# Three groups of products and the residual stream with tokens on partitions instead of features

## The chip, the core and the metric

One core of a Trainium2 chip runs the whole program; the other cores are idle. The metric is the device time of one execution in microseconds (us). The engines have short names: PE is TensorE's matrix products, PEld its loads of standing tiles, DVE is VectorE, ACT is ScalarE, POOL is GpSimd, SP is the queue that issues the weight loads.

## What is computed

Two layers of an encoder over 256 tokens of 2048 features, all float32. Each layer reads the residual stream x twice and adds to it twice:

```python
for l in range(DEPTH):                       # DEPTH = 2
    u = rmsnorm(x, norm_mix[l])
    proj = u @ w_in[l]
    c_q, c_kv, k_pe, q_na, k_na, v_na, gate_a, gate_b = jnp.split(proj, IN_SPLITS, axis=-1)
    ...                                      # latent attention and neighbourhood attention
    y_a = mla_attention(...) @ w_o_mla[l]    # 1024 -> 2048
    y_b = neighbourhood_attention(...) @ w_o_na[l]
    merged = jax.nn.sigmoid(gate_a) * y_a + jax.nn.sigmoid(gate_b) * y_b
    x = x + merged @ w_out[l]                # 2048 -> 2048
    h = rmsnorm(x, norm_mlp[l]) @ w_ff1[l]   # 2048 -> 8192
    x = x + jnp.square(jax.nn.relu(h)) @ w_ff2[l]   # 8192 -> 2048
return rmsnorm(x, norm_final)
```

## The kernel before

An activation is held with features on partitions: 128 features by 256 tokens, split exactly into a float32r part hi and the rest lo, side by side in one tile of 512 columns (`pair`, L76; `split`, L140). A weight is loaded in strips of two times 128 rows by 512 columns (`weights`, L149): one load of 1 MB on SP's queue for two strips, then ACT makes the hi part of a strip (L164) and DVE the lo part (L165). There are three buffers for loads and four for split strips. Every product is the sum of hi times hi, hi times lo and lo times hi.

`gemm_b` (L210) makes 512 output features from all rows of a weight. The weight's 128 by 128 tile stands in the array and the activation streams past it: one instruction with the weight's hi and 512 columns (hi and lo of the 256 tokens, L186) and one with the weight's lo and 256 columns (L187). I call these two **a pair**; a strip is eight pairs, in four blocks m of 128 output features. The two halves of the result are added by ACT and DVE (`whole`, L203), and `evac` uses the sum. Banks of PSUM: five for products, three (`abank`) for attention, transposes and norms.

`mm_a` (L192) is the other way round, used before only for the values v: a 128 by 128 tile of the activation (hi or lo, one block t of 128 tokens) stands and 512 columns of the weight stream past it, in three instructions (L194 to L196), **a triple**. The result has tokens on partitions and nothing is left to add.

x is kept as 16 tiles `xT` of features by tokens. Its first transposes are those of the input (`enter`, L393), its last those of the output (`turned`, L572). RMSNorm's scale of a token is applied to a product's result as a row `mix.row` or `mlp.row` along the free axis, which `Norm.scales` (L241) makes with small products (L245, L259).

The order on each engine is set by a scheduler that simulates the program while it is built; the program hands it work in the order in which it is written. Steps of attention heads and norms are generators: `tick()` (L111), called after each block of a product, advances one of them when its lag has passed, and `drain()` runs all that is left. Engines work in order, so what stands at the head of an engine's row holds up what is behind it.

Of the kernel before, what the change touches and what calls it, by code (L numbers as in the profile page):

```python
# [44 lines left out]
# columns of w_in  # L45
# [3 lines left out]
# columns of the gains' tile  # L49
G_MIX, G_MLP, G_FIN, G_QA, G_KVA, G_ALL = 0, 2 * NC, 4 * NC, 5 * NC, 5 * NC + 8, 5 * NC + 16  # L50

# buffers: operands of 2 KiB a partition, PSUM banks for attention, small temporaries, loaded
# strips of weights, split ones
NSLOT, ABANKS, SMALL, RBUFS, HBUFS = 47, 3, 8, 3, 4
# steps of a large product: between an attention head's start and the next one's, after its
# scores, after its transposes
# [4 lines left out]
def trunk(ctx: ExitStack, tc: tile.TileContext, x, w_in, w_uq, w_ukv, rpb, w_o_mla, w_o_na,  # L61
          w_out, w_ff1, w_ff2, gains, cos, sin, turns, halves, mask, out):
# [42 lines left out]
    xT = [const.tile([P, S], F32, name=f"xT{c}") for c in range(NC)]  # L105
# [34 lines left out]
    def split(dst, src, scale=1.0):  # L140
        """dst[:, :256] = float32r(src * scale), dst[:, 256:] = src * scale - that."""
# [26 lines left out]
    def weights_twice(w, nk, c0, n):  # L168
        """All rows of columns c0.. of w, each column twice over, eight times 128 rows a strip."""
# [19 lines left out]
    def mm_d(ps, wh, wl, a, first, last):  # L189
        mm_3(ps[:, :S], wh, wl, a[:, :S], a[:, S:], first, last)  # L190

    def mm_a(ps, a, t, wh, wl, first, last):  # L192
        """ps = a(token block t).T @ weights."""
# [16 lines left out]
    def gemm_b(w, c0, acts, evac, before=None, ahead=None, direct=False):  # L210
# [15 lines left out]
    class Norm:  # L226
# [14 lines left out]
        def scales(self, rows=True):  # L241
# [9 lines left out]
            if not rows:  # L251
                return
# [442 lines left out]
```

## Time and profile before

| | us |
|---|---|
| time, median of 3 runs | 2723.74 (2723.41 to 2723.89) |
| span of the profiled execution, first to last instruction | 2721.4 |
| PE busy in it | 2700.0 |
| PEld busy | 2363.2 |
| DVE busy | 1741.9 |
| ACT busy | 1408.5 |

The page gives no time of its own for the profiled execution, only its span; the runs' median lies 2.3 us above that. PE's busy time is made of instructions that overlap, so how long one takes is read from the distance between starts, and not from its own length.

### The profile page before, as it was taken

How to read it: one execution, taken by the hardware profiler on the slowest of the kernel's cores; microseconds unless marked ns; L12 is line 12 of the kernel's file. 1: busy time of each engine (PE TensorE's matmuls, PEld its weight loads, DVE VectorE, ACT ScalarE, POOL GpSimd, SP SyncE). 2: the span in 40 equal slices, each digit the busy share in tenths (PEclk: the TensorE clock that was granted, in tenths of full speed). 3: DMA queues.
4: the chain of work that ended last, by engine and by line, in shares of the span. 5: the costliest groups of instructions: out<-in, count | busy, mean ns of one | idle time of the engine just before them, and what ended most of it. 6: DMA issues, size and time to landing. Idle time of an engine off the chain costs nothing.

```text
span 2721.4 us, 39453 instructions
## 1 busy us (share of the span) xinstructions
PE 2700.0 (99%) x15608; PEld 2363.2 (87%) x15608; DVE 1741.9 (64%) x2649; ACT 1408.5 (52%) x2279; POOL 125.0 (5%) x153
## 2 busy tenths in 40 slices
PE   8999999999999999999999999999999999999998
PEld 7888898888888888888888888988888888888887
DVE  6676587666656556556667765876666556565564
ACT  5555465555544445445555554655555454454554
POOL 3110000001000000000101100000100000000001
PEclk9999999999999999999999999999999999999999
DMA  7555544555555555555555555455555555556553
GB/s 228 182 172 185 185 159 155 186 171 187 187 200 179 199 190 179 194 184 187 187 186 182 168 181 183 132 186 186 186 186 186 189 183 195 177 186 201 174 198 124
DMA packets 253545, 495.78 MB, mean 182 GB/s; under 512 B 12625, under 2 KB 16721, under 8 KB 253361
## 3 DMA queue, kind: packets, MB, share of 16 engines
q1 hardware_dynamic: 250624, 488.14, 54.8%
q0 software_dynamic: 1728, 3.51, 0.5%
q8 instruction: 122, 2.00, 0.3%
q10 hardware_dynamic: 1008, 1.62, 0.2%
q14 instruction: 63, 0.51, 0.1%
HBM read 491.14 MB, written 2.10 MB: 181 GB/s over the span
## 4 chain that ended last, share of the span: by engine, by line
PE 97%; issue 1%; DVE 1%; DMA 0%; ACT 0%; POOL 0%; POOLq 0%; ACTq 0%; DVEq 0%
PE bank L186 60%; PE bank L187 30%; PE bank L194 1%; PE bank L195 1%; PE bank L196 1%; PE abank L200 1%; PE abank L199 1%; PE abank L201 1%; PE abank L303 1%; DVE lo L165 0%; DMA raw<-in_w_in 0%; PE abank L273 0%; DMA wide<-in_x 0%; PE abank L401 0%; PE abank L259 0%
## 5 line engine op out<-in xcount | busy, mean ns | idle before, releaser
L186 PE MATMUL bank<-pair,hi 128*128 128x512 f32 x7040 | 2443.3, 397 | 4.2 <-DVE pair L146 3.9
L187 PE MATMUL bank<-pair,lo 128*128 128x256 f32 x7040 | 1893.0, 281 | 0.0
L165 DVE TENSOR_TENSOR lo<-raw,hi 128x1024 fp32r<-128x1024 f32 (+1 forms) x928 | 1122.3, 1222 | 804.0 <-ACT hi L164 801.6
L186 PEld LDWEIGHTS bank<-pair,hi 128*128 128x128 f32 x7040 | 1306.3, 188 | 282.6 <-DVE pair L146 4.2
L164 ACT CAST hi<-raw 128x1024 fp32r<-128x1024 f32 (+1 forms) x928 | 956.6, 1047 | 956.0 <-PE bank L186 888.1
L187 PEld LDWEIGHTS bank<-pair,lo 128*128 128x128 f32 x7040 | 1330.9, 189 | 35.1 <-DVE lo L165 0.2
L207 DVE TENSOR_TENSOR small<-bank,small 128x256 f32<-128x256 f32 x502 | 198.1, 418 | 54.8 <-ACT small L205 51.9
L205 ACT COPY small<-bank 128x256 f32<-128x256 f32 x502 | 180.9, 364 | 40.5 <-PE bank L187 39.9
L239 POOL TENSOR_TENSOR acc<-acc,small 128x256 f32<-128x256 f32 x83 | 70.7, 852 | 2293.6 <-ACT small L238 2293.2
L142 ACT ACTIVATE pair<-small 128x256 fp32r<-128x256 f32 x232 | 93.7, 418 | 41.6 <-DVE small L328 22.1
L607 ACT ACTIVATE small<-small 128x256 f32<-128x256 f32 x128 | 53.3, 416 | 98.9 <-DVE small L605 98.9
L144 DVE TENSOR_TENSOR pair<-small,pair 128x256 fp32r<-128x256 f32 x200 | 81.8, 419 | 33.1 <-ACT pair L142 33.1
L195 PE MATMUL bank<-lo,pair 128*128 128x512 f32 (+1 forms) x192 | 68.8, 358 | 0.0
L196 PE MATMUL bank<-hi,pair 128*128 128x512 f32 (+1 forms) x192 | 68.0, 354 | 0.0
L194 PE MATMUL bank<-hi,pair 128*128 128x512 f32 (+1 forms) x192 | 67.7, 356 | 0.0
L558 DVE TENSOR_TENSOR xT<-xT,small 128x256 f32<-128x256 f32 x144 | 56.4, 421 | 2.3
L605 DVE SCALAR_TENSOR_TENSOR small<-small,rrow 128x256 f32<-128x256 f32 x128 | 53.9, 421 | 1.1
L142 ACT ACTIVATE pair<-xT,g_sb 128x256 fp32r<-128x256 f32 x48 | 24.4, 507 | 44.3 <-DVE xT L558 44.3
L146 DVE SCALAR_TENSOR_TENSOR pair<-xT,g_sb,pair 128x256 fp32r<-128x256 f32 x48 | 28.7, 604 | 19.1 <-ACT pair L142 19.1
L194 PEld LDWEIGHTS bank<-hi,pair 128*128 128x128 f32 x192 | 36.2, 189 | 5.4
L196 PEld LDWEIGHTS bank<-hi,pair 128*128 128x128 f32 x192 | 36.3, 189 | 5.0
L195 PEld LDWEIGHTS bank<-lo,pair 128*128 128x128 f32 x192 | 36.3, 189 | 4.8
(111 smaller groups left out, 931.3 us busy)
## 6 DMA issues: line engine op xcount, KB each, us to landing
raw<-in_w_ff SPq DMA_DIRECT2D x256, 1024.0 KB, 5.4
raw<-in_w_in SPq DMA_DIRECT2D x124, 1024.0 KB, 5.3
raw<-in_w_out SPq DMA_DIRECT2D x32, 1024.0 KB, 5.1
raw<-in_w_o_na SPq DMA_DIRECT2D x16, 1024.0 KB, 5.1
raw<-in_w_o_mla SPq DMA_DIRECT2D x16, 1024.0 KB, 5.0
raw<-in_w_ukv SPq DMA_DIRECT2D x8, 1024.0 KB, 5.1
raw<-in_w_uq SPq DMA_DIRECT2D x8, 768.0 KB, 4.7
raw<-in_w_in SPq DMA_DIRECT2D x10, 512.0 KB, 5.1
```

What stands on the lines that cost most here:

```text
L142: nc.scalar.activation(dst[:, :S], src, AF.Copy, scale=scale)
L144: nc.vector.tensor_tensor(dst[:, S:], src, dst[:, :S].bitcast(F32), op=ALU.subtract)
L164: nc.scalar.copy(hi, src)
L165: nc.vector.tensor_tensor(lo, src, hi.bitcast(F32), op=ALU.subtract)
L186: nc.tensor.matmul(ps, wh, a, start=first, stop=False)
L187: nc.tensor.matmul(ps[:, :S], wl, a[:, :S], start=False, stop=last)
L194: nc.tensor.matmul(ps, a[:, t * P:(t + 1) * P], wh, start=first, stop=False)
L195: nc.tensor.matmul(ps, a[:, t * P:(t + 1) * P], wl, start=False, stop=False)
L196: nc.tensor.matmul(ps, a[:, S + t * P:S + (t + 1) * P], wh, start=False, stop=last)
L205: nc.scalar.copy(h, ps[:, S:])
L207: nc.vector.tensor_tensor(t, ps[:, :S], h, op=ALU.add)
L239: (engine or nc.gpsimd).tensor_tensor(self.acc, self.acc, sq, op=ALU.add)
```

## The change

The gates (columns `C_GA`, `C_GB` of `w_in`), `w_o_na`, `w_o_mla`, `w_out` and `w_ff2` go through a new `gemm_a`, which uses triples; `w_ff1` and the other columns of `w_in` stay with pairs. x is two tiles `xt` of 128 tokens by 2048 features. The gated sum and x are turned by PE (`turned`, 128 by 128 blocks, four into one `abank`) where the next product needs features on partitions. Sums of squares of x come from ACT along the free axis (`RowNorm`). The MLP's scale is no longer applied to each hidden block but, squared, where `w_ff2`'s result is added to x. There are 44 instead of 47 slots for operands.

```diff
+    xt = [const.tile([P, D], F32, name=f"xt{t}") for t in range(2)]
...
+    def gemm_a(w, c0, acts, evac):
+
+        nk = len(acts)
+        ps = [bank() for _ in range(2)]
+        for k0, wh, wl in weights(w, nk, c0, 512):
+            for t in range(2):
+                for k in range(k0, k0 + 2):
+                    mm_a(ps[t], have(acts, k), t, wh[:, k - k0], wl[:, k - k0], k == 0, k == nk - 1)
+                tick()
+        for t in range(2):
+            evac(t, ps[t])
...
+    class RowNorm:
...
+        def add(self, t, c4):
+            junk = tmp.tile([P, 512], F32, tag="junk", name="junk", bufs=1)
+            nc.scalar.activation(junk, xt[t][:, c4 * 512:(c4 + 1) * 512], AF.Square,
+                                 accum_out=self.sums[:, t, c4:c4 + 1])
...
+    def turned(src, c4, dst, scale):
+
+
+        for c in range(0, 4, 2):
+            tp = abank()
+            for i in range(2):
+                for t in range(2):
+                    nc.tensor.transpose(tp[:, (2 * i + t) * P:(2 * i + t + 1) * P],
+                                        src(t)[:, (c + i) * P:(c + i + 1) * P], ident)
+            for i in range(2):
+                a = pair()
+                split(a, tp[:, i * S:(i + 1) * S], scale(4 * c4 + c + i))
+                dst[4 * c4 + c + i] = a
+            yield 1
...
-            gemm_b(wi, C_GB + c4 * 512, xg, gate(th))
+            gemm_a(wi, C_GB + c4 * 512, xg, gate(th))
...
-            gemm_b(w_o_na[l], c4 * 512, att_na, merge)
+            gemm_a(w_o_na[l], c4 * 512, att_na, merge)
...
+                nc.vector.scalar_tensor_tensor(th[t], th[t], 1.0, ps, op0=ALU.add, op1=ALU.mult)
+                nc.vector.tensor_tensor(m, m, th[t], op=ALU.add)
+                if t == 1:
+                    start(turned(lambda t, c4=c4: part[t, c4], c4, mg, lambda c: 0.5), 2)
...
+                cs = xt[t][:, c4 * 512:(c4 + 1) * 512]
+                if scale is None:
+                    nc.vector.tensor_tensor(cs, cs, ps, op=ALU.add)
+                else:
+                    nc.vector.scalar_tensor_tensor(cs, ps, scale.sq[:, t:t + 1], cs, op0=ALU.mult, op1=ALU.add)
...
-            gemm_b(w_out[l], c4 * 512, mg, residual(c4, mlp, G_MLP + l * NC, xg))
-        start(mlp.scales(), 10)
+            gemm_a(w_out[l], c4 * 512, mg,
+                   residual(c4, None, mlp, lambda c4, xg=xg: turned_x(c4, xg, G_MLP + l * NC)))
+        start(mlp.square(), 10)
...
-                nc.vector.scalar_tensor_tensor(t, t, 0.0, mlp.row, op0=ALU.max, op1=ALU.mult)
-                r = small()
-                nc.scalar.activation(r, t, AF.Square)
+                nc.vector.scalar_tensor_tensor(t, t, 0.0, t, op0=ALU.max, op1=ALU.mult)
...
-                gemm_b(w_ff2[l][b * D:(b + 1) * D, :], c4 * 512, hid, ev,
-                       direct=last and b == NB - 1 and c4 == 3)
+                gemm_a(w_ff2[l][b * D:(b + 1) * D, :], c4 * 512, hid, ev)
...
+            nc.vector.scalar_tensor_tensor(o, xt[t][:, cs], norm.col[:, t:t + 1], gfin[c4],
+                                           op0=ALU.mult, op1=ALU.mult)
```

The first place is PE where the second of `w_out`'s four products begins (first layer). Before, its first strip on bank 5943:

```order
L187 MATMUL bank_5731<-pair_5725,lo_5881 128x256
L186 MATMUL bank_5943<-pair_4726,hi_5949 128x512
L187 MATMUL bank_5943<-pair_4726,lo_5950 128x256
L186 MATMUL bank_5943<-pair_4735,hi_5949 128x512
L187 MATMUL bank_5943<-pair_4735,lo_5950 128x256
L186 MATMUL bank_5943<-pair_4744,hi_5969 128x512
```

After, the same place, banks 5079 and 5080 being the two blocks of tokens:

```order
L201 MATMUL bank_4914<-hi_5057,pair_4962 128x512
L199 MATMUL bank_5079<-hi_5083,pair_4223 128x512
L200 MATMUL bank_5079<-lo_5084,pair_4223 128x512
L201 MATMUL bank_5079<-hi_5083,pair_4223 128x512
L199 MATMUL bank_5079<-hi_5083,pair_4226 128x512
L200 MATMUL bank_5079<-lo_5084,pair_4226 128x512
L201 MATMUL bank_5079<-hi_5083,pair_4226 128x512
```

Pairs of 512 and 256 columns have become triples of 512. In its second strip, after 21 instructions of the new product, PE now turns the 512 columns of x that the product before has just finished:

```order
L200 MATMUL bank_5080<-lo_5111,pair_4244 128x512
L201 MATMUL bank_5080<-hi_5110,pair_4244 128x512
L326 MATMUL abank_5099<-ident_70,xt0_91 128x128
L326 MATMUL abank_5120<-ident_70,xt0_91 128x128
L199 MATMUL bank_5080<-hi_5110,pair_4247 128x512
L326 MATMUL abank_5099<-ident_70,xt1_92 128x128
L326 MATMUL abank_5099<-ident_70,xt0_91 128x128
L326 MATMUL abank_5099<-ident_70,xt1_92 128x128
L326 MATMUL abank_5120<-ident_70,xt1_92 128x128
L326 MATMUL abank_5120<-ident_70,xt0_91 128x128
L326 MATMUL abank_5120<-ident_70,xt1_92 128x128
```

Eight transposes stand in one block there, of which there was none before. The second place is DVE at the end of the same product (bank 5079 and 5080 after, 5943 to 5946 before). Before, each of four blocks is added up, added to x and split:

```order
L165 TENSOR_TENSOR lo_6208<-raw_6205,hi_6207 128x1024
L207 TENSOR_TENSOR small_6117<-bank_5943,small_6115 128x256
L558 TENSOR_TENSOR xT4_95<-xT4_95,small_6117 128x256
L165 TENSOR_TENSOR lo_6228<-raw_6205,hi_6227 128x1024
L146 SCALAR_TENSOR_TENSOR pair_6120<-xT4_95,g_sb_79,pair_6120 128x256
L207 TENSOR_TENSOR small_6128<-bank_5944,small_6126 128x256
L558 TENSOR_TENSOR xT5_96<-xT5_96,small_6128 128x256
```

After:

```order
L173 TENSOR_TENSOR lo_5277<-raw_5247,hi_5276 128x1024
L173 TENSOR_TENSOR lo_5306<-raw_5303,hi_5305 128x1024
L617 TENSOR_TENSOR xt0_91<-xt0_91,bank_5079 128x512
L617 TENSOR_TENSOR xt1_92<-xt1_92,bank_5080 128x512
L173 TENSOR_TENSOR lo_5322<-raw_5303,hi_5321 128x1024
L173 TENSOR_TENSOR lo_5340<-raw_5337,hi_5339 128x1024
L154 SCALAR_TENSOR_TENSOR pair_5270<-abank_5265,g_sb_79,pair_5270 128x256
```

Two additions of 512 columns (L617) have taken the place of eight operations of 256 (L207 and L558 for each of four blocks). Three strips of the next product are split ahead of them, and the splits of the turned blocks (L154) come after two more. The third place is ACT at the program's start, where `xT` and `xt` hold x. Before:

```order
L93 DMA g_sb<-in_gains 128x96
L142 ACT_TABLE_LOAD
L142 ACTIVATE pair<-abank,g_sb 128x256 x2
L391 DMA wide<-in_x 128x512 x2
L142 ACTIVATE pair<-abank,g_sb 128x256
L164 CAST hi<-raw 128x1024
```

After:

```order
L95 DMA g_sb<-in_gains 128x80
L462 DMA xt_91<-in_x 128x512
L462 DMA xt_92<-in_x 128x512
L296 ACT_TABLE_LOAD
L296 ACTIVATE junk,sums<-xt_91 128x512
L462 DMA xt_91<-in_x 128x512
L296 ACTIVATE junk,sums<-xt_92 128x512
L150 ACTIVATE pair<-abank,g_sb 128x256
```

Two of ACT's six loads of x now go ahead of its table load, and two sums of squares stand ahead of the first split.

## Rows read from the trace of the kernel before

**Rows 1.** The page: span, then busy time, share of the span and instructions of each engine.

```profile
span 2721.4 us, 39453 instructions
PE 2700.0 (99%) x15608; PEld 2363.2 (87%) x15608; DVE 1741.9 (64%) x2649; ACT 1408.5 (52%) x2279; POOL 125.0 (5%) x153
```

**Rows 2.** The page: the chain that ended last, shares of the span by engine.

```profile
PE 97%; issue 1%; DVE 1%; DMA 0%; ACT 0%; POOL 0%; POOLq 0%; ACTq 0%; DVEq 0%
```

**Rows 3.** Stretches: length, busy us (instructions) by engine, granted clock, DMA share, GB/s.

```profile
64.00:81.00 17.00, 17.00 (x80) 14.18 (x80) 11.29 (x19) 8.47 (x13) 0.00 (x0) 1.00 0.60 192
277.10:355.70 78.60, 78.60 (x451) 68.47 (x450) 46.77 (x68) 39.35 (x60) 0.00 (x0) 1.00 0.55 178
553.00:642.60 89.60, 89.60 (x514) 78.17 (x513) 59.93 (x84) 47.46 (x74) 8.67 (x11) 1.00 0.57 191
733.40:823.00 89.60, 89.60 (x514) 78.16 (x513) 51.31 (x69) 41.93 (x58) 0.00 (x0) 1.00 0.57 187
1002.70:1092.90 90.20, 90.20 (x515) 78.56 (x514) 54.30 (x77) 45.24 (x70) 0.00 (x0) 1.00 0.57 188
```

**Rows 4.** Timeline of PE, values of heads 0 to 3: start, length, instruction.

```profile
65.00 0.40 PE L194 MATMUL bank<-hi,pair 128*128 128x512 f32 x1
...
66.39 0.39 PE L194 MATMUL bank<-hi,pair 128*128 128x512 f32 x1
...
76.84 0.40 PE L195 MATMUL bank<-lo,pair 128*128 128x512 f32 x1
...
87.29 0.39 PE L186 MATMUL bank<-pair,hi 128*128 128x512 f32 x1
```

**Rows 5.** Timeline of PE around four transposes of an attention head.

```profile
98.13 0.40 PE L186 MATMUL bank<-pair,hi 128*128 128x512 f32 x1
...
98.84 0.60 PE L303 MATMUL abank<-ident,p 128*128 128x128 f32 x4
...
99.98 0.40 PE L186 MATMUL bank<-pair,hi 128*128 128x512 f32 x1
```

**Rows 6.** Timeline of PE around the small products of a norm.

```profile
200.49 0.39 PE L186 MATMUL bank<-pair,hi 128*128 128x512 f32 x1
200.72 0.50 PE L245 MATMUL abank<-ones,acc 128*128 128x2 f32 x4
...
201.28 0.40 PE L186 MATMUL bank<-pair,hi 128*128 128x512 f32 x1
```

**Rows 7.** Timeline of PE and ACT at the start; idle time and what ended it in brackets.

```profile
8.80 2.08 PE L186 MATMUL bank<-pair,hi 128*128 128x512 f32 x4 [0.26 <-ACT hi L164]
20.57 0.50 PE L186 MATMUL bank<-pair,hi 128*128 128x512 f32 x1 [3.93 <-DVE pair L146]
41.00 0.39 PE L186 MATMUL bank<-pair,hi 128*128 128x512 f32 x1
17.35 1.05 ACT L164 CAST hi<-raw 128x1024 fp32r<-128x1024 f32 x1 [1.75 <-DMA raw<-in_w_in]
```

**Rows 8.** Timeline of PE and of SP's queue at the end.

```profile
2708.14 0.28 PE L199 MATMUL bank<-pair,hi 128*128 128x256 f32 x1
2708.50 0.28 PE L199 MATMUL bank<-pair,hi 128*128 128x256 f32 x1
2708.74 0.29 PE L201 MATMUL bank<-pair,lo 128*128 128x256 f32 x1
2713.08 4.49 SPq L637 DMA_DIRECT2D out<-wide  x8
```

**Rows 9.** Groups by line and shape: busy us, mean ns of one, idle before.

```profile
L165 DVE TENSOR_TENSOR lo<-raw,hi 128x1024 fp32r<-128x1024 f32 x912 | 1107.2, 1227 | 797.8 <-ACT hi L164 795.4 <-PE bank L187 1.0
L321 DVE SCALAR_TENSOR_TENSOR vl<-bank,rcol,vh 128x512 fp32r<-128x512 f32 x8 | 6.0, 748 | 1.9 <-ACT vh L320 1.9
L320 ACT ACTIVATE vh<-bank,rcol 128x512 fp32r<-128x512 f32 x8 | 5.5, 690 | 3.9 <-PE bank L196 3.9
L303 PE MATMUL abank<-ident,p 128*128 128x128 f32 x128 | 20.1, 272 | 0.0
```

More of the change, by code (lines that the diff above doesn't have):

```diff
@@ L61, in trunk @@
 def trunk(ctx: ExitStack, tc: tile.TileContext, x, w_in, w_uq, w_ukv, rpb, w_o_mla, w_o_na,
-          w_out, w_ff1, w_ff2, gains, cos, sin, turns, halves, mask, out):
+          w_out, w_ff1, w_ff2, gains, gain_fin, cos, sin, turns, halves, mask, out):
     nc = tc.nc
@@ L224, in gemm_b, with rows_of, root @@
             evac(m, ps[m])
+    def rows_of(col):
+        dg = [tmp.tile([P, P], F32, tag="diag", name="diag", bufs=4) for _ in range(2)]
+        for t in range(2):
+            nc.vector.tensor_scalar_mul(dg[t], ident, col[:, t:t + 1])
+        yield 5
+        pb = abank()
+        for t in range(2):
+            nc.tensor.matmul(pb[:, t * P:(t + 1) * P], ones, dg[t], start=True, stop=True)
+        row = tmp.tile([P, S], F32, tag="rrow", name="rrow", bufs=4)
+        nc.vector.tensor_copy(row, pb[:, :S])
+        return row
+    def root(v, width, name):
+        nc.vector.tensor_scalar(v, v, 1.0 / width, EPS, op0=ALU.mult, op1=ALU.add)
+        col = tmp.tile([P, 2], F32, tag="rcol", name=name, bufs=6)
+        nc.gpsimd.tensor_tensor(col, v, mhalf, op=ALU.pow)
+        return col
     class Norm:
@@ L256, in scales, with __init__, scale, square @@
-            yield 5
-            pb = abank()
-            for t in range(2):
-                nc.tensor.matmul(pb[:, t * P:(t + 1) * P], ones, dg[t], start=True, stop=True)
-            self.row = row = tmp.tile([P, S], F32, tag="rrow", name="rrow", bufs=3)
-            nc.vector.tensor_copy(row, pb[:, :S])
+            nc.vector.tensor_copy(v, ps[:, 0:4:2])
+            self.col = root(v, self.width, "col")
+            self.row = yield from rows_of(self.col)
+    class RowNorm:
+        def __init__(self):
+            self.sums = tmp.tile([P, 2, 4], F32, tag="sums", name="sums", bufs=2)
+        def add(self, t, c4):
+            junk = tmp.tile([P, 512], F32, tag="junk", name="junk", bufs=1)
+            nc.scalar.activation(junk, xt[t][:, c4 * 512:(c4 + 1) * 512], AF.Square,
+                                 accum_out=self.sums[:, t, c4:c4 + 1])
+        def scale(self):
+            v = tmp.tile([P, 2], F32, tag="var", name="var", bufs=2)
+            nc.vector.tensor_reduce(v, self.sums, axis=AX.X, op=ALU.add)
+            self.col = root(v, D, "col")
+        def scales(self):
+            self.scale()
+            self.half = tmp.tile([P, 2], F32, tag="rcol", name="half", bufs=6)
+            nc.vector.tensor_scalar_mul(self.half, self.col, 0.5)
+            self.row = yield from rows_of(self.col)
+        def square(self):
+            self.scale()
+            self.sq = tmp.tile([P, 2], F32, tag="rcol", name="sq", bufs=6)
+            nc.vector.tensor_tensor(self.sq, self.col, self.col, op=ALU.mult)
+            return
+            yield
@@ L397, in enter @@
             load(k0 // 2)
-        for c in (k0, k0 + 1):
-            tp = abank()
+        if k0 % 4 == 0:
+            enter.gen = turned_x(k0 // 4, xg, G_MIX)
             for t in range(2):
-                nc.tensor.transpose(tp[:, t * P:(t + 1) * P],
-                                    xin[t, c // 4][:, (c % 4) * P:(c % 4 + 1) * P], ident)
-            xg[c] = pair()
-            split(xg[c], tp[:, :S], g_sb[:, G_MIX + c:G_MIX + c + 1])
-            nc.vector.tensor_copy(xT[c], tp[:, :S])
-            norm.add(xT[c])
+                norm.add(t, k0 // 4)
+        next(enter.gen)
     for l in range(DEPTH):
@@ L546, in trunk @@
+            gemm_a(wi, C_GA + c4 * 512, xg, gate(th))
             if c4 == 0:
                 drain()
[L548 to L561 removed]
+            gemm_a(w_o_mla[l], c4 * 512, att, merge)
@@ new lines, in trunk, with residual, evac @@
+        last = l == DEPTH - 1
+        def residual(c4, scale=None, n=None, then=None):
+            def evac(t, ps):
+                cs = xt[t][:, c4 * 512:(c4 + 1) * 512]
[3 more added lines that the diff above has]
+                    nc.vector.scalar_tensor_tensor(cs, ps, scale.sq[:, t:t + 1], cs, op0=ALU.mult, op1=ALU.add)
+                if n is not None:
+                    n.add(t, c4)
+                if then is not None and t == 1:
+                    start(then(c4), 2)
+            return evac
@@ L585, in final @@
-        def final(c4):
-            ts = []
-            def evac(m, ps):
-                c = 4 * c4 + m
-                t = tmp.tile([P, S], F32, tag="th", name="th", bufs=4)
-                ts.append(t)
-                nc.vector.tensor_tensor(t, xT[c], whole(ps) if c4 < 3 else ps[:, :S], op=ALU.add)
-                norm.add(t, nc.vector if c4 == 3 else None)
-                nc.scalar.activation(t, t, AF.Copy, scale=g_sb[:, G_FIN + c:G_FIN + c + 1])
-                if m == 3:
-                    start(turned(c4, ts), 10)
-            return evac
```

134 lines of the change are left out of this document (46 added, 88 removed).

## The prediction, made before the changed kernel had run

> **What bounds the kernel now.** I read the busy times first: PE 99% of the span, DVE 64%, ACT 52% [rows 1]. That PE is always busy doesn't yet say that it sets the end, so the chain that ended last comes next: PE holds 97% of it [rows 2]. Then the stretches, for the distance between starts. They show PE busy for the whole of each, at a granted clock of 1.00 (2.4 GHz), in gates with `w_o_na`, in `w_out`, in `w_ff2` and in `w_ff1` [rows 3]. No product waits for a load, a split or a bank outside the start and the end, so the time is the sum of what PE's instructions take, one after another, plus a start and an end. Work taken off DVE, ACT and POOL is worth nothing here, and work added to PE costs its full length.
>
> **Products, the main term.** A pair and half a triple do the same work: 768 columns for 128 features, 128 of the sum and 256 tokens. A strip has eight pairs or four triples. What a pair takes is a stretch divided by its pairs: 89.60 us for 256 in `w_ff2` and in `w_out` is 0.350 us each, 78.60 for 224 in gates and `w_o_na` is 0.351, 90.20 for 256 in `w_ff1` is 0.352 [rows 3] (a stretch counts one or two instructions more, those that overlap its edges). What a triple takes can be read in this very kernel, from the values v, in the same loop with the same tiles: from 76.84 to 87.29 there are 46 instructions of 512 columns, 0.2272 us each, so 0.6815 a triple [rows 4]. Two pairs take 0.700. The gain is 0.019 per triple, since three instructions start where four did.
>
> How many: a layer's gates are 8 products of 16 times 128 rows, `w_o_na` and `w_o_mla` 8 of 8, `w_out` 4 of 16, `w_ff2` 16 of 16, together 512 times 128 rows, 1024 in two layers: 2048 triples. Before, these are 4032 pairs, and in the last product 64 groups of three with 256 columns, 0.36 us each (2708.14 to 2708.50) [rows 8]. Before: gates and outputs 1536 x 0.3509 = 539.0, `w_out` 512 x 0.350 = 179.2, `w_ff2` 1984 x 0.350 = 694.4, the last 64 x 0.36 = 23.0, sum 1435.6. After: 2048 x 0.6815 = 1395.7. **Minus 39.9 us.** Bounds: in the first six instructions of the values, where the stage before is still being added up, an instruction takes (66.39 - 65.00) / 6 = 0.232 [rows 4]; if all were like that, the gain is 1435.6 - 6144 x 0.232 = 10 us. I take the long run, because the long products have few such starts.
>
> The Trainium skill has a rule that speaks against this ("TensorE: Matmul & The Clock Gate", section "Back-to-back issue gap"): started back to back, a warm matmul of N columns takes N / 2.4 ns and 2.5 ns more. By it two pairs take 650 ns and a triple 648, and the whole term would be an estimated 5 us instead of 39.9. The trace doesn't bear it out: 227 ns where the rule has 216, and 350 for a pair where it has 325.
>
> **Transposes.** New ones: 64 for the gated sum, 64 for x ahead of `w_ff1`, 32 for x ahead of layer 1, 160 in all, in 20 blocks of eight; the 32 of the input stay. Their price is a whole number of pairs around four of them: from 98.13 to 99.98 there are four pairs (1.408) and four transposes, 1.85 in all, so 0.11 each [rows 5]. Plus 17.6. Of the 32 that go (`turned` of before) 24 lie between products: minus 2.6; eight lie in the end. The profile gives one transpose a length of 272 ns [rows 9], but they start much closer together than that. The Trainium skill (same page, "Part 4: PE-mode transpose") puts one at about 275 ns in a kernel: as a length the trace agrees, as a cost it doesn't; 160 x 0.275 would be 44 us, and the forecast 26 us later.
>
> **Small products of norms.** Four L245 between 200.49 and 201.28 with one pair: 0.79 - 0.352 = 0.44, 0.11 each [rows 6]. Gone between products: 16 of L245 (sums for four norms) and 8 of L259 (the rows of the MLP's scale, taken at the same price). Minus 2.6.
>
> **The start.** The first product runs from 8.80 to 41.00 [rows 7]; its 64 pairs and 24 transposes need 22.5 + 2.6, so some 7 us are lost there, 3.93 of them in one wait for a split on DVE, behind ACT, which stood at a cast that waited for a weight load until 17.35 [rows 7]. After, two loads of x go earlier and 16 copies leave DVE, but two sums of squares stand ahead of ACT's first split, and eight more transposes ahead of the first product. It can come out either way, from 5 us less (most of the loss gone) to 3 more (a strip of weights behind 0.5 MB of x; a 1 MB strip pair takes 5.5 us at 192 GB/s [rows 3]). I take minus 2.0.
>
> **The end.** Before, 4.1 us pass from the end of the last product (2709.0) to the first output DMA, and the rest to 2721.4 is the writing of 2 MB [rows 8]. After: the last residual on DVE 0.75, squares on ACT 0.69 (rows with 512 columns: L321, L320 [rows 9]), three small steps, one output of 0.75: about 3.5 to 4.5. DVE makes all eight outputs, 0.75 apart; the writing takes (2721.4 - 2713.1) / 8 = 1.04 apart, so it stays the slower. Taken as nothing, between 1.5 less and 1.5 more.
>
> **What is costed at nothing, and its cover.** A block of eight transposes waits for DVE to add the second half of the tokens, and PE works in order, so all products are queued behind it. In `w_out` 21 instructions of 0.227 stand between the end of the product before and the block: 4.8 us. DVE needs the end of one split (1.23 [rows 9]) and one addition (0.75), 2 us. At the beginning of `w_ff1` there are 11 pairs, 3.9 us; behind the gated sum, where DVE has four operations (3.0 and 1.23), 27 instructions, 6.1 us. The cover holds by 1.7 us at the least. The gates' and residuals' additions fall into DVE's idle third [rows 1] and leave its row with fewer operations than before. The loads stay 481 in the same order on SP; a strip lasts 2.73 instead of 2.80 us, so the demand rises from 188 to 193 GB/s, which the values' stage already draws (192, at a DMA share of 0.60 [rows 3]). The final gain's four loads on POOL's queue have a whole block of the MLP to land.
>
> **The sum.** -39.9 + 17.6 - 2.6 - 2.6 - 2.0 = -29.5 us. On the span of 2721.4 this gives 2691.9; the median of the runs lies 2.3 above the span, carried over unchanged: **2694 us**, 1.1% faster.
>
> **Rivals.** First, the blocks of transposes wait after all. It needs DVE to be two splits later than I count (2.5 us, against a cover of 1.7), as when a split stands in front of the addition and waits for a load. Then each of the 20 blocks costs 0.8: 16 us, 2710, still faster. For it: PE has nothing else in its row. Against it: the addition stands ahead of the fourth strip's split in DVE's order, and that split can't be needed earlier.
>
> Second, on the other side: a product takes time by its columns alone, so a triple lasts as long as two pairs (0.700) and the values' 0.6815 belongs to their short stretch, where the weights' splits run ahead. Then the main term is nothing and the transposes remain: 17.6 - 2.6 - 2.6 - 2.0 = +10.4, 2734. It decides from 0.693 a triple on: below that the gain covers the transposes. The skill's rule cited above comes to nearly this. For it: `w_ff2` runs four such products on end, the values one. Against it: four stretches of values, in two layers, all alike.
>
> Third, the change doesn't do what it says because the weights arrive no faster: if the loads can't exceed 188 GB/s for long, PE waits for strips and the products keep their old time, again 2734. Against it: DMA share 0.57 [rows 3].
>
> **How the numbers follow.** Forecast 0.75, first rival 0.14, second 0.07, third 0.04. The predicted time is the forecast's. Its own bounds: -5 and +3 for the start, 1.5 for the end, and 0.2275 to 0.230 for an instruction in place of 0.2272 if starts weigh more (+2 to +17); below, 0.2265 would give -4. I take 2682 to 2712; it holds the first rival and leaves out the other two and the far end of the prices, somewhat under 2 in 10. A measurement tells 0.2% (5.4 us) from no change, so faster means below 2718.3: forecast and first rival all but their far ends, 0.88; within 0.2%: 0.04; slower, the second and third rival mostly: 0.08.
>
> **What the profile will show.** PE's instructions fall from 15608 by some 2000. In `w_ff2` the starts of triples lie 0.227 apart; at 0.233 the second rival holds. The blocks of eight take 0.9 us with no idle time ahead of them; idle time put down to DVE's `xt` there is the first rival. DVE and ACT fall well below 64% and 52% with no effect. The first product ends near 39. DMA rises to some 185 GB/s on average. The forecast is wrong if PE shows idle time inside the products.

## The result, and the profile after

The changed kernel takes 2689.51 us (median of 4 runs, 2689.2 to 2689.91), the kernel before 2723.57 in the same comparison (2723.01 to 2723.89): a ratio of 0.9876, 95% interval 0.9862 to 0.989. That is 34.1 us less, where 29.5 had been forecast (2694).

The page of the changed kernel: span, busy time by engine, and the chain that ended last.

```profile
span 2688.1 us, 34037 instructions
PE 2666.8 (99%) x13596; PEld 2268.7 (84%) x13596; DVE 1602.9 (60%) x2158; ACT 1277.1 (48%) x1815; POOL 60.5 (2%) x86
...
PE 84%; issue 14%; DVE 1%; DMA 1%; ACT 0%; POOL 0%; SPq 0%; POOLq 0%; DVEq 0%; ACTq 0%
```

Beside [rows 1, 2]: PE has 2012 instructions fewer and is as full as before. The chain shows 14% as "issue", time in which an engine waits for nothing that the profile shows; that this isn't idle time is seen from the waits below.

Stretches: length, busy us (instructions) by engine in the order PE, PEld, DVE, ACT, POOL, granted clock, DMA share, GB/s. They are gates and `w_o_na`; gates and `w_o_mla`; `w_out`; a block of `w_ff2`; a block of `w_ff1`.

```profile
218.70:350.70 132.00, 132.00 (x589) 109.43 (x588) 68.30 (x72) 57.12 (x62) 2.20 (x3) 1.00 0.58 189
404.90:547.14 142.24, 142.24 (x676) 118.94 (x675) 83.48 (x110) 67.80 (x98) 0.00 (x0) 1.00 0.53 174
547.14:637.84 90.70, 90.70 (x418) 75.33 (x416) 51.54 (x59) 43.79 (x60) 0.00 (x0) 1.00 0.54 186
728.70:815.76 87.06, 87.06 (x386) 72.10 (x385) 46.94 (x50) 35.37 (x37) 0.00 (x0) 1.00 0.57 191
815.76:905.43 89.67, 89.67 (x513) 78.10 (x512) 52.64 (x72) 42.51 (x59) 0.00 (x0) 1.00 0.57 189
```

A block of `w_ff2` is 384 instructions of 512 columns in 87.06 us, 0.2267 each, where [rows 3] has 89.60 for 256 pairs. `w_out` is longer than before although its products are shorter: its transposes are in it. `w_ff1` is issued in the same form as before and is yet 0.5 shorter, which the prediction did not forecast.

All waits of PE that the trace lists: where PE waited, for what, us in total, times, longest.

```profile
PE abank L326 <- DMA xt<-in_x: 7.4, 3, 4.5
PE bank L194 <- DVE small L212: 1.0, 2, 0.5
PE bank L194 <- ACT hi L172: 1.0, 2, 0.7
PE bank L195 <- DVE lo L173: 0.3, 1, 0.3
PE bank L194 <- DVE pair L154: 0.3, 1, 0.3
```

All but the two of 0.5 us lie in the first 34 us. So behind the start the time is, as before, the sum of PE's own instructions.

PE around a block of eight transposes in `w_out` (L326), among triples (L199 to L201): start, length, instruction.

```profile
597.02 0.40 PE L201 MATMUL bank<-hi,pair 128*128 128x512 f32 x1
597.25 0.38 PE L326 MATMUL abank<-ident,xt 128*128 128x128 f32 x2
597.39 0.48 PE L199 MATMUL bank<-hi,pair 128*128 128x512 f32 x1
597.70 0.82 PE L326 MATMUL abank<-ident,xt 128*128 128x128 f32 x6
598.28 0.48 PE L200 MATMUL bank<-lo,pair 128*128 128x512 f32 x1
```

From 597.25 to 598.28 there are eight transposes and one product: 1.03 - 0.227 = 0.80 us, 0.10 a transpose, and no idle time stands in brackets.

The start: PE's first product with what ended the idle time ahead of it, PE at the first instruction of the next product, then ACT's first split of a weight strip.

```profile
12.32 2.07 PE L194 MATMUL bank<-pair,hi 128*128 128x512 f32 x4 [0.71 <-ACT hi L172]
...
41.45 0.39 PE L194 MATMUL bank<-pair,hi 128*128 128x512 f32 x1
...
11.22 1.04 ACT L172 CAST hi<-raw 128x1024 fp32r<-128x1024 f32 x1 [1.37 <-DMA raw<-in_w_in]
```

Against [rows 7] the first product starts 3.52 us later, because ACT waits for the first strip until 11.22, and ends 0.45 later.

The end: PE's last product, DVE's eight outputs and their issue on SP's queue.

```profile
2676.53 0.39 PE L201 MATMUL bank<-hi,pair 128*128 128x512 f32 x1
...
2679.76 5.39 DVE L670 SCALAR_TENSOR_TENSOR wide<-xt,col,wide 128x512 f32<-128x512 f32 x8 [0.83 <-POOL col L259]
...
2680.53 4.97 SPq L672 DMA_DIRECT2D out<-wide  x8
```

From the end of the last product (2676.92) to the first output are 3.6 us (4.1 before), and from there to the end 7.6 (8.3 before, [rows 8]).

By stages, with what the terms of the prediction give for each (us of the span, both layers together; lengths between starts on PE):

| stage | before | after | forecast | measured |
|---|---|---|---|---|
| start, to the end of the first product | 41.00 | 41.45 | -2.0 | +0.5 |
| second product and values of heads 0 to 3 | 46.29 | 44.88 | -0.4 | -1.4 |
| gates and `w_o_na`, x2 | 136.00 | 132.00 | -7.8 | -8.0 |
| latent attention, x2 | 54.00 | 54.21 | 0 | +0.4 |
| gates and `w_o_mla`, x2 | 143.30 | 142.24 | -2.5 | -2.1 |
| `w_out`, x2 | 89.66 | 90.70 | +2.3 | +2.1 |
| `w_ff1`, first block, x2 | 90.80 | 90.86 | 0 | +0.1 |
| `w_ff1`, the other blocks, x6 | 90.12 | 89.67 | 0 | -2.7 |
| `w_ff2`, six blocks | 89.60 | 87.06 | -14.2 | -15.2 |
| last block of `w_ff2` in layer 0 and first product of layer 1 | 112.96 | 113.51 | +0.6 | +0.6 |
| last block of `w_ff2` and end | 105.76 | 98.45 | -5.6 | -7.3 |

The last column adds up to -33.0 of the spans' difference of -33.3; the rest is rounding and the stages left out, which are alike within 0.1. Of the transposes, the 32 of a layer's gated sum lie in the stage of `w_o_mla` (24) and in `w_out` (8), and the 32 of x ahead of `w_ff1` in `w_out` (24) and in `w_ff1`'s first block (8).

### The profile page after: what moved, and what is told of

It is laid out like the page before. It is cut to its first block, busy times and chain, and to the rows that moved or that the text cites. A ratio compares the mean times of both kernels' runs of the same rounds, so it can differ in the third digit from the quotient of the medians.

```text
span 2688.1 us, 34037 instructions
## 1 busy us (share of the span) xinstructions
PE 2666.8 (99%) x13596; PEld 2268.7 (84%) x13596; DVE 1602.9 (60%) x2158; ACT 1277.1 (48%) x1815; POOL 60.5 (2%) x86
## 3 DMA queue, kind: packets, MB, share of 16 engines
q0 software_dynamic: 2048, 4.56, 0.6%
## 4 chain that ended last, share of the span: by engine, by line
PE 84%; issue 14%; DVE 1%; DMA 1%; ACT 0%; POOL 0%; SPq 0%; POOLq 0%; DVEq 0%; ACTq 0%
PE bank L194 21%; PE bank L199 16%; PE bank L200 16%; PE bank L201 16%; PE bank L195 11%; DMA raw<-in_w_in 1%; PE abank L206 1%; PE abank L205 1%; PE abank L204 1%; PE abank L326 1%; PE abank L377 0%; DVE lo L173 0%; DVE wide L670 0%; PE abank L347 0%; ACT hi L172 0%
## 5 line engine op out<-in xcount | busy, mean ns | idle before, releaser
L194 PE MATMUL bank<-pair,hi 128*128 128x512 f32 x3008 | 1059.0, 398 | 2.3 <-DVE small L212 1.0
L200 PE MATMUL bank<-lo,pair 128*128 128x512 f32 (+1 forms) x2240 | 866.1, 387 | 0.0
L199 PE MATMUL bank<-hi,pair 128*128 128x512 f32 (+1 forms) x2240 | 865.8, 388 | 0.0
L201 PE MATMUL bank<-hi,pair 128*128 128x512 f32 (+1 forms) x2240 | 865.8, 387 | 0.0
L195 PE MATMUL bank<-pair,lo 128*128 128x256 f32 x3008 | 835.5, 280 | 0.4 <-DVE lo L173 0.3
L194 PEld LDWEIGHTS bank<-pair,hi 128*128 128x128 f32 x3008 | 563.5, 188 | 133.0 <-ACT hi L172 1.9
L195 PEld LDWEIGHTS bank<-pair,lo 128*128 128x128 f32 x3008 | 567.7, 189 | 5.9 <-DVE lo L173 1.6
L201 PEld LDWEIGHTS bank<-hi,pair 128*128 128x128 f32 x2240 | 420.8, 188 | 84.6
L199 PEld LDWEIGHTS bank<-hi,pair 128*128 128x128 f32 x2240 | 420.8, 188 | 84.1
L200 PEld LDWEIGHTS bank<-lo,pair 128*128 128x128 f32 x2240 | 420.9, 188 | 82.6
L210 ACT COPY small<-bank 128x256 f32<-128x256 f32 x218 | 78.6, 369 | 29.0 <-PE bank L195 27.8
L212 DVE TENSOR_TENSOR small<-bank,small 128x256 f32<-128x256 f32 x218 | 83.0, 416 | 0.2
L154 DVE SCALAR_TENSOR_TENSOR pair<-abank,g_sb,pair 128x256 fp32r<-128x256 f32 x64 | 29.2, 478 | 23.0 <-ACT pair L150 23.0
L150 ACT ACTIVATE pair<-abank 128x256 fp32r<-128x256 f32 x64 | 23.6, 381 | 29.2 <-PE abank L206 19.1
```

The lines of the kernel that those rows point to most:

```text
L150: nc.scalar.activation(dst[:, :S], src, AF.Copy, scale=scale)
L199: nc.tensor.matmul(ps, a[:, t * P:(t + 1) * P], wh, start=first, stop=False)
L200: nc.tensor.matmul(ps, a[:, t * P:(t + 1) * P], wl, start=False, stop=False)
L201: nc.tensor.matmul(ps, a[:, S + t * P:S + (t + 1) * P], wh, start=False, stop=last)
L210: nc.scalar.copy(h, ps[:, S:])
L212: nc.vector.tensor_tensor(t, ps[:, :S], h, op=ALU.add)
```

## The experiments

Theory: PE's time is the sum of its instructions, each of which costs something for its start beside its columns; three long ones for four mixed ones is the gain, and the transposes are paid back out of it at 0.1 us each, unhidden and without a wait. Rivals: columns alone count; the transposes wait, or hide. Then three questions on what the forecast had missed: `w_ff1`, the start, the end. Each experiment is compared with the 2689.51 us of the changed kernel; beside the experiments the kernel before had medians of 2723.3 to 2723.8, so a difference under some 0.5 us says nothing. The edits are shown shortened, with `...` or words for what is left out.

### Triples issued in halves

```diff
-        nc.tensor.matmul(ps, ah, wh, ...); (ps, ah, wl); (ps, al, wh)
+        for x, w in ((ah, wh), (ah, wl), (al, wh)):
+            for h in range(2):
+                nc.tensor.matmul(ps[:, h * S:(h + 1) * S], x, w[:, h * S:(h + 1) * S], ...)
```

> Changed kernel, but w_ff2's triples, except the first of each product and block of tokens, are issued as six instructions of 256 columns instead of three of 512: 960 triples, the same columns and the same standing tiles. Theory (an instruction start costs time of its own, so fewer and longer instructions are what the change gains by): six instructions of 256 columns at 0.12 us, the distance in the last product of the kernel before, are 0.72 us against 0.680, times 960: about +38 us, from +29 (0.1185 each) to +55 (0.123). Rival (a product takes time by its columns alone): 0 us. By the Trainium skill, page TensorE: Matmul & The Clock Gate, section Back-to-back issue gap, three more starts of 2.5 ns would be an estimated +7 us.

2730.74 us, 41.2 more, slower than the kernel before (1.0027, 1.0017 to 1.0037). The first triple of each product and block of tokens stays whole here, so 960 of 1024 are halved. The same block of `w_ff2` as above, in the same order of figures, then PE's timeline within it:

```profile
727.90:819.80 91.90, 91.90 (x746) 90.81 (x745) 47.04 (x51) 35.09 (x38) 0.00 (x0) 1.00 0.56 183
```

```profile
762.28 0.64 PE L221 MATMUL bank<-hi,pair 128*128 128x256 f32 x4
762.76 0.40 PE L221 MATMUL bank<-lo,pair 128*128 128x256 f32 x2
```

Four starts in 0.48 us, 0.120 each, at the same granted clock of 1.00; a block takes 4.8 us more. The rival of columns alone falls: the columns are the same, only the number of instructions has risen, and more than the whole gain of the change is gone. The two lengths together give the price: 0.2267 us for 512 columns and 0.120 for 256 leave 0.1067 for 256 columns, which is 2.4 GHz, and 0.0133 for each start. PEld is busy for 90.81 of the 91.90 us, so one could think that the loads of standing tiles set the 0.120; but transposes load a tile each as well and start 0.109 apart in their rows of six and eight, so a load alone isn't the 0.120. For transposes the price of a start is too low: 128 columns at 2.4 GHz and one start would be 0.067. So columns and a start give the time at 256 and 512 columns, and not at 128; why, no run here asked.

### Transposes twice, and none

```diff
-                    nc.tensor.transpose(tp[...], src(t)[...], ident)
+                    for _ in range(2):
+                        nc.tensor.transpose(tp[...], src(t)[...], ident)
```

> Changed kernel, but each of the 160 transposes that stand between products is issued twice in a row into the same place. Theory (a transpose in PE's row costs 0.11 us and nobody waits for the block): +17.6 us. Rival (a transpose costs its length of 272 ns): +43.5 us. Rival (the transposes hide behind the products' weight loads): 0.

```diff
-            tp = abank(); four transposes into tp; split(a, tp[:, i * S:(i + 1) * S], ...)
+            split(a, src(i)[:, c * P:(c + 2) * P], ...)
```

> Changed kernel without the 160 transposes between products: the splits read 128 by 256 blocks of the rows with tokens on partitions straight from SBUF, so features and tokens are not exchanged there and the products multiply other numbers; the input's 32 transposes stay. Theory (the blocks cost PE their own time and no wait): -17.6 us. Rival (PE waits for DVE ahead of the 20 blocks, 0.8 each): -33 us. Rival (hidden): 0.

Twice: 2705.31, 15.8 more, 0.099 a transpose. None: 2670.42, 19.1 less, 0.119 each. PE with the doubled block, now sixteen in a row, between triples:

```profile
601.61 1.91 PE L327 MATMUL abank<-ident,xt 128*128 128x128 f32 x16
603.28 0.48 PE L199 MATMUL bank<-hi,pair 128*128 128x512 f32 x1
```

1.67 us for sixteen, 0.104 each. Both runs fit the theory's 0.11 within some 10% and exclude 272 ns each, hidden transposes and waits of 0.8 us at every block. That leaving out saves somewhat more than doubling costs may be the splits' work and the order around the blocks, which change too; 3 us of such effects aren't taken apart.

### Gates back to pairs, and w_ff1 turned as well

```diff
-            gemm_a(wi, C_GB + c4 * 512, xg, gate(th))
+            gemm_b(wi, C_GB + c4 * 512, xg, gate(th))
```

(in the same way `C_GA`, `w_o_na` and `w_o_mla`, with the sums of before)

> Changed kernel, but the gates, w_o_na and w_o_mla are issued as pairs again, with features on partitions, and the gated sum isn't turned. Theory by the terms of the prediction: 1536 pairs at 0.3509 against 768 triples at 0.6815 is +15.6 us, 64 transposes less at 0.11 is -7.0, together +8.6; by the lengths of the same stages in the two profiles (136.00 against 132.00 and 143.30 against 142.24 in each layer) +10.1. Rival (columns alone): only the transposes count, -7 us.

```diff
-                gemm_b(w_ff1[l], b * D + c4 * 512, xg, relu2)
+                gemm_a(w_ff1[l], b * D + c4 * 512, xg, relu2)
...
+                    if t == 1:
+                        start(turned(lambda t: rows[t], c4, hid, lambda c: 1.0), 2)
```

> Changed kernel, and w_ff1 is issued as triples too, with the hidden block turned by PE, 256 more transposes in all. Theory (a triple saves 0.019 us, a transpose costs 0.10 to 0.11, so turning pays only where many products share it): -20 for 1024 triples and +25 to +28 for the transposes, together +5 to +8 us. Rival (triples are better wherever they go): -20 us or so. Rival (PE waits for the blocks of the hidden, since w_ff2 needs them at once): +20 us or more, with idle time on PE.

Gates back: 2697.80, 8.3 more: this part of the change was worth that, as its terms say. `w_ff1` turned: 2697.07, 7.6 more than without. PE's groups there, by form:

```profile
L199 PE MATMUL bank<-hi,pair 128*128 128x512 f32 x3200 | 1253.3, 392 | 0.0
...
L326 PE MATMUL abank<-ident,wide 128*128 128x128 f32 x320 | 46.9, 272 | 0.0
```

No idle time stands ahead of the 320 transposes of hidden blocks and gated sums (last column), so it's their own time: at the prices found above, 1024 triples save some 20 us and 256 transposes cost some 27, which makes the 7.6. Triples aren't better wherever they go. A transpose costs 0.1 us and a triple saves 0.02, so a transpose must buy five triples. In `w_ff1` it would buy four; in the change as it stands 160 transposes go with 2048 triples, 13 each.

### The 0.45 us of w_ff1

The kernel before squared a hidden block on ACT; the changed one lets DVE do it in one step. Three edits, each around `relu2`:

```diff
-                nc.vector.scalar_tensor_tensor(t, t, 0.0, t, op0=ALU.max, op1=ALU.mult)
-                split(a, t)
+                nc.vector.scalar_tensor_tensor(t, t, 0.0, t, op0=ALU.max, op1=ALU.max)
+                r = small()
+                nc.scalar.activation(r, t, AF.Square)
+                split(a, r)
```

> Changed kernel, but the square of a hidden block is made by ACT again as in the kernel before (DVE takes the larger of the value and 0, ACT squares it), 256 operations of 128 by 256 more on ACT. It asks why the seven later blocks of w_ff1, whose products are issued in the same form by both kernels, take 89.67 us instead of 90.12. Theory (PE's pairs run a little slower beside more work of ACT and DVE): blocks of w_ff1 back at about 90.1, in all +2.7 to +3.6 us. Rival (the difference comes with something else, such as the freed slots or the other scale): blocks stay at 89.67, 0 us.

```diff
                 nc.vector.scalar_tensor_tensor(t, t, 0.0, t, op0=ALU.max, op1=ALU.mult)
+                extra(t)          # a square on ACT into a buffer of its own
```

> Changed kernel with 512 operations added on ACT that nothing waits for: one square of 128 by 256 beside each hidden block of w_ff1 (256 in all) and eight beside the end of each product of w_ff2 (256). Theory (pairs run slower beside more work of another engine, whatever it is for): the later blocks of w_ff1 at 90.2 us instead of 89.67, as with the square back on ACT. Rival (it was the longer way to the hidden pair that counted): 89.67. For w_ff2's triples, which start 226.7 ns apart almost without scatter: 87.07 if they aren't touched by it, 87.6 if they are touched like pairs. In all about +3.5 us, 0 by the rival, or +7.

The first: 2692.96, 3.4 more, all of it in `w_ff1`. The second: 2692.29, 2.8 more, but in another place: eight spare squares stand ahead of the last norm, and the last block with the end is 101.41 instead of 98.45. A block of `w_ff1` in the first, then a block of `w_ff2` and one of `w_ff1` in the second:

```profile
993.15:1083.35 90.20, 90.20 (x513) 78.46 (x512) 52.94 (x72) 44.95 (x69) 0.00 (x0) 1.00 0.55 188
```

```profile
905.52:992.58 87.06, 87.06 (x386) 72.07 (x385) 46.99 (x50) 46.02 (x65) 0.00 (x0) 1.00 0.58 193
992.58:1082.25 89.67, 89.67 (x514) 78.07 (x513) 52.72 (x72) 49.23 (x79) 0.00 (x0) 1.00 0.56 189
```

With the square back on ACT the block is at 90.20, as in the kernel before (90.12). With 49.23 us of work on ACT instead of 44.95 it stays at 89.67: it isn't the load of ACT that slows PE, and my theory fell. Two more edits asked whether it is the rotation of buffers:

```diff
                 nc.vector.scalar_tensor_tensor(t, t, 0.0, t, op0=ALU.max, op1=ALU.mult)
+                r = small()
+                nc.scalar.activation(r, t, AF.Square)      # read by nobody
```

> Changed kernel with one square of 128 by 256 on ACT beside each hidden block of w_ff1, as with the square back on ACT, written into a buffer of the same pool, but read by nobody: the hidden pair is made from DVE's result as in the changed kernel. Squares that nobody waits for, written to a place of their own, had left w_ff1's blocks at 89.67 us. Theory (the rotation of buffers, and so the places in memory, decides): 90.2, in all +3.5. Rival (it is the order of PE's instructions, which the longer chain from DVE over ACT to the pair brings about: 30 groups of two or more 256-column instructions in a row in a block of w_ff1 instead of 3): 89.67, 0 us in all, as long as PE's order stays alternating.

```diff
-                nc.vector.scalar_tensor_tensor(t, t, 0.0, t, op0=ALU.max, op1=ALU.mult)
+                r = small()
+                nc.vector.scalar_tensor_tensor(r, t, 0.0, t, op0=ALU.max, op1=ALU.mult)
+                t = r
```

> Changed kernel in which DVE writes the squared hidden block into another buffer of the pool instead of in place, one buffer more for each block and no instruction more. Theory (the rotation of buffers decides): w_ff1's later blocks at 90.2 us, +3.5 in all. Rival (order of PE's instructions, or ACT's place in the chain): 89.67, 0.

2691.88 and 2689.80, 2.4 and 0.3 more. A block of `w_ff1` in each:

```profile
991.94:1082.18 90.24, 90.24 (x514) 78.48 (x512) 53.78 (x72) 44.50 (x69) 0.00 (x0) 1.00 0.56 188
```

```profile
991.53:1081.32 89.79, 89.79 (x513) 78.18 (x512) 52.62 (x72) 41.19 (x57) 0.00 (x0) 1.00 0.56 189
```

A square that nobody reads, in a buffer of the rotating pool, slows the pairs fully in the later blocks (the two first blocks are 0.42 shorter with it, so that 2.4 us are left of 3.4); the rotation without the square hardly does (89.79), and the square without the rotation not at all. So the longer chain to the hidden pair isn't needed. The rival of PE's order isn't settled, for the order changed in the slower forms too: over such a block the groups of two and more 256-column instructions in a row are 3 in the changed kernel (89.67), 30 with the square back (90.20), 27 with the unread square (90.24), but 24 with the other buffer (89.79), and 3 with the square in a place of its own (89.67). The number of such groups alone doesn't give the time, but which instructions they join may. What shows itself is that a 512-column instruction between two of 256 takes 236.1 ns in the mean instead of 234.2. Why, stays open; square and rotation were seen to bring it about together, with PE's order changed in the same run, and 2.7 us of the 34 hang on it.

### The start and the end

```diff
-            queue = nc.sync if c4 == 0 else nc.scalar
-            queue.dma_start(xt[t][...], x[...])
+            nc.sync.dma_start(xt[t][...], x[...])
```

> Changed kernel, but all eight loads of x go on SP's queue, in turn with the first four strips of weights, so that the first strip isn't issued behind or beside the second half megabyte of x. Theory (the first strip landed at 11.2 us instead of 7.7 because that load shared the transfers): first product's start at 9 to 10 instead of 12.32, its end at 38 to 39.5 instead of 41.45, and 2 to 3 us off the time. Rival (the first product is held by the bytes of x and weights together, or by DVE's splits, and not by their order): end at 41 to 42, no change.

2687.81, 1.7 less than the changed kernel. ACT's first split of a strip, then PE's first product and the waits that came in its place:

```profile
7.20 1.04 ACT L172 CAST hi<-raw 128x1024 fp32r<-128x1024 f32 x1 [0.45 <-DMA raw<-in_w_in]
...
8.93 2.06 PE L194 MATMUL bank<-pair,hi 128*128 128x512 f32 x4
...
24.34 0.38 PE L195 MATMUL bank<-pair,lo 128*128 128x256 f32 x1 [1.05 <-DVE lo L173]
...
38.35 0.39 PE L194 MATMUL bank<-pair,hi 128*128 128x512 f32 x1
...
39.92 0.39 PE L195 MATMUL bank<-pair,lo 128*128 128x256 f32 x1 [0.17 <-DVE lo L173]
...
41.34 0.39 PE L195 MATMUL bank<-pair,lo 128*128 128x256 f32 x1 [0.46 <-DVE lo L173]
```

The strip is there 4 us earlier, the product starts 3.4 earlier and ends at 38.35 instead of 41.45, as the theory has it. But the second product then takes 1.1 us longer, 0.6 of it in the waits for splits on DVE shown here, and by the end of the values 2.0 us are left of the 3.1; in the time it is 1.7, less than the 2 to 3 expected. One trace is not quite enough for differences of this size: in the nine other traces of experiments that keep the changed kernel's start, the first strip comes between 10.95 and 12.03 and the first product ends between 40.28 and 41.32. The 38.35 here and the 38.55 of the next run lie clear of them. So the order of the loads was the cause of the late start, and behind it DVE's splits are a part of what holds the next product.

```diff
+                if pre and c4 < 3:
+                    nc.vector.tensor_tensor(cs, cs, gfin[c4], op=ALU.mult)     # ahead of the last norm
...
+            if c4 == 3: (DVE as before)  elif t == 0: nc.vector.tensor_scalar_mul(o, xt[t][:, cs], col)
+            else: nc.scalar.activation(o, xt[t][:, cs], AF.Copy, scale=col)
+            queue = nc.scalar if t == 1 and c4 < 3 else nc.sync
```

> The kernel with x on SP's queue, and another end: the rows of x that are final early are multiplied by the final gain while PE still works, so that after the last norm only the token's scale is left, and ACT makes and sends three of the eight outputs. Theory (the outputs are 0.664 us apart because DVE makes all eight): last product's end to the end of the program 8 to 9 us instead of 11.2, so 2 to 3 us less than with x on SP's queue alone. Rival (the writing of 2 MB sets it): no change of the end.

2687.98, no better than with x on SP's queue alone (2687.27 to 2688.75). DVE's outputs, and the two queues' issues:

```profile
2677.15 1.28 DVE L676 TENSOR_SCALAR wide<-xt,col 128x512 f32<-128x512 f32 x3 [0.83 <-POOL col L259]
...
2677.66 3.46 SPq L680 DMA_DIRECT2D out<-wide  x5
...
2678.51 1.34 ACTq L680 DMA_DIRECT2D out<-wide  x2
```

And the outputs' groups of issues, KB each and the median from issue to landing, changed kernel first:

```profile
out<-wide SPq DMA_DIRECT2D x8, 256.0 KB, 2.1
```

```profile
out<-wide SPq DMA_DIRECT2D x5, 256.0 KB, 3.8
...
out<-wide ACTq DMA_DIRECT2D x3, 256.0 KB, 3.4
```

All eight are issued within 3.5 us instead of 5, and each takes longer to land: from the first issue to the end of the span (2685.7) 8.0 us, against 7.6 in the changed kernel. The theory had 8 to 9 us from the last product's end to the end of the span; it is 11.4, and 11.2 in the changed kernel. The writing of 2 MB sets the end, as the rival has it: DMA's share is 1.02 at 395 GB/s from 2682 to 2686 in the changed kernel and 1.05 at some 403 from 2679.6 to 2683.6 here. In the changed kernel the two limits are about even: outputs are issued 0.66 us apart and land 0.65 apart, so the writing keeps up with DVE; here they land 0.70 apart.

## Why the prediction was right, point by point

**Products: right.** A triple was put at 0.6815 us from the values' stage; it takes 0.680 in `w_ff2` (87.06 / 128). -39.9 had been forecast; the stages that hold nothing else agree, `w_ff2` -15.2 for -14.2 and gates with `w_o_na` -8.0 for -7.8. The second rival (columns alone) is refuted by the halved triples, and the reason is now known more closely: two pairs start four times and a triple three times, which is 0.0133 us; the rest of the 0.02 is that a mixed pair takes 0.350 where 768 columns and two starts make 0.347. The rule of the Trainium skill weighed in the prediction (TensorE: Matmul & The Clock Gate, section Back-to-back issue gap) is right that a start costs time beside the columns; this case's trace has 13.3 ns where the Trainium skill has 2.5, for 256 and 512 columns and products whose every instruction loads its own standing tile.

**Transposes: right, perhaps slightly dear.** 0.11 was forecast, 0.10 measured in the block, between 0.099 and 0.119 by doubling and leaving out. The first rival (waits at the blocks) did not come: no idle time stands ahead of L326 but the input's 7.4 us at the start. The cover was a little better than the prediction says: its own figures leave at least 1.9 us (3.9 - 2.0 and 6.1 - 4.2), not 1.7, which makes that rival 0.6 a block and 12 us.

**Norms' small products: right** in the sum, but the stage of the second product gained 1.4 us for a forecast of 0.4: four more small products (0.44) have moved ahead into the first product, and a wait of 0.30 for POOL's sum (L239 of the kernel before), which stood ahead of the four L245 that are gone, is gone with them. The rest lies within the scatter: the stage takes 44.8 to 45.6 in the traces that keep this start.

**The start: the term failed.** -2.0 was taken between -5 and +3; it was +0.5, of which 0.44 are the four small products moved there, and -0.7 to +0.3 in the nine other traces with this start. The step that failed is the one from "two loads of x go earlier" to a gain. The prediction had seen that a strip might stand behind 0.5 MB of x and yet took a value on the side of the gain. The first strip came at 11.22, and with the loads in another order the forecast end of 39 is met (38.35).

The prediction also counted "some 7 us" of the start before as lost and named a wait for 3.93 of them. Most of the other 3 was the clock. The kernel before, by engine as above, with the granted clock third from the end:

```profile
20.00:25.00 5.00, 4.43 (x17) 3.88 (x18) 5.00 (x9) 2.88 (x6) 3.41 (x3) 0.68 0.69 195
```

Behind the idle time of 3.93 the trace has a granted clock of 0.50 (1.2 GHz) from 21.82 to 25.23; and up to 11.6 PE took its first pairs at half pace too. At half pace for 2.8 and 3.4 us, PE loses about 3. The changed kernel has its own such stretch, from 12.32 to 18.24 (the last section), so this loss was not there to be won.

**The end: right in the main, the size off by 1.2 us.** The writing bounds it, as the end with faster outputs shows. But the prediction's 1.04 us an output was too dear: they land 0.65 apart, no slower than DVE makes them (0.66), and the eight take 7.6 us instead of 8.3; they come evenly from one engine, and the first is 0.45 us earlier. "Taken as nothing" was off by less than its own bounds of 1.5.

**Costed at nothing, but not nothing: `w_ff1`, -2.7.** "Work taken off DVE, ACT and POOL is worth nothing here" failed there, though not because ACT is lighter: pairs with the same operands took 0.352 us before (90.20 for 256 in [rows 3]) and 0.350 after. The prediction took a pair's price in this stage for one that the form of instruction fixes; it moved by half a per cent.

**New and unforeseen: two waits of 0.51 us** in latent attention, where PE needs a bank that DVE's addition (L212) has yet to read. They're the whole +0.4 of that stage.

Right for its reasons, then, in the two terms that carry it; the misses (start +2.5, second product -1.0, `w_ff1` -2.7, six blocks of `w_ff2` -1.0, last block and end -1.7) went mostly one way and leave the span 3.8 us below the 2691.9 forecast for it; the other 0.7 of the 4.5 by which the time lies below 2694 is the 2.3 between span and median, carried over unchanged. Of the signs named ahead, PE's count, 0.227 us between starts, blocks without idle time, DMA at 185 GB/s and the missing effect of the engines beside PE hold; "the first product ends near 39" does not, and DVE (60%) and ACT (48%) fell only by four points each. The 481 loads on SP's queue are 470 of weights in both traces, 480 issues with two loads of x and the outputs. The third rival (loads no faster than 188 GB/s) is refuted by the 191 in `w_ff2` without a wait.

## What to carry to other kernels

Where PE is full from end to end, count its instructions and not only its columns: 512 columns took 0.227 us and 256 took 0.120, so the operand that can stream 512 wide should stream, and the narrower one stand. A turn of the layout by PE is paid in full (0.1 us for 128 by 128), so turn what many products share, the residual stream or a sum, and leave what only a few share. What is loaded first at the start, and how much the last write has to move, set the ends; another engine and queue at work on the outputs did nothing.

## What the runs showed of the hardware

- A start costs 13.3 ns beside the columns at 256 and 512 columns, with a standing tile loaded for each, even where two instructions in a row use the same one (745 loads for 746 products in the halved block). Transposes of 128 columns start 0.109 us apart, more than that price gives.
- In the first 18 us PE takes its products at half the pace of later: from 15.26 to 16.11 one of 512 columns and two of 256, 0.85 us for 1024 columns, as at 1.2 GHz, in a stretch for which the profile's view gives a granted clock of 1.00 (12 to 19 us). PE had stood idle for 4.5, 1.9, 1.0 and 0.7 us in between until 12.32; from 19.9 on a 512-column instruction starts 0.24 us ahead of the next. The trace's first record of the granted clock begins at 18.24, at 1.00; ahead of it there is none, and the view shows 1.00 there for want of a record. So at a program's start the distance between starts tells the clock, and the column doesn't. In the nine other traces with this start the first record lies between 15.3 and 18.1. PE's timeline in the changed kernel there:

```profile
15.26 0.63 PE L194 MATMUL bank<-pair,hi 128*128 128x512 f32 x1
15.68 0.63 PE L195 MATMUL bank<-pair,lo 128*128 128x256 f32 x2
16.11 0.63 PE L194 MATMUL bank<-pair,hi 128*128 128x512 f32 x1
```

And the stretch, with the granted clock third from the end:

```profile
12.00:19.00 7.00, 6.42 (x20) 5.04 (x20) 2.58 (x3) 3.28 (x8) 1.01 (x1) 1.00 0.97 290
```

- Triples hardly scatter (nearly all starts of a block of `w_ff2` lie 226 or 227 ns apart), whatever ACT does beside them; pairs scatter between 223 and 242 ns for the 512-column instruction, and by block lengths they moved by 0.6% (89.67 to 90.24) between kernels that issue the same ones in partly another order.
